# A hybrid decoder step on one core: which engine issues the last stores of the mLSTM and of the prompt attention, and which engine reads out the attention's last result

## The chip, the cores and the metric

The kernel runs on one core of one Trainium2 chip. The metric is the time of the core on the device in microseconds (us), as the median of several executions. The profile is of one execution, with its own time.

## The reference

One inference step of a decoder layer, for a new sequence of 2048 tokens ("prompt") and for 8 x 8 new tokens with a paged past of 8192 positions each ("sample"). Cut to what matters:

```python
z = x @ w_in                                   # one projection for everything
fq, fk, fv, flogf = heads of z                 # FoX attention: 8 heads of 64
mq, mk, mv, ig, lf, og = heads of z            # mLSTM: 4 heads of 128, after a short convolution
fox_h = softmax(fq fk^T / 8 + L_i - L_j, causal) fv     # L = cumulative log forget gate
(C, n, m), m_h = scan over chunks of the mLSTM # matrix memory C, normaliser n
mn  = norm(m_h) * mlstm_norm_w * sigmoid(og)
x1  = layer_norm(ALPHA * x + concat(fox_h, mn) @ w_o)
y   = layer_norm(ALPHA * x1 + relu(x1 @ w1)^2 @ w2)
return y, keys, values, log forget values, C, n, m, convolution state  (prompt and sample)
```

All in 32-bit floats. The kernel gives a product of two 32-bit operands as three products of their high and low parts.

## The kernel before

The program is one long stream of tiles; each engine gets a queue of its own, and a planner of the library orders each engine's queue before the run by its own model of the times (program order is a priority there, not a rule). At run time each queue is in order: an instruction that waits holds up everything behind it on its engine. That includes the instructions that issue DMAs: SyncE (SP in the profile) issues most of them, ScalarE (ACT) and GpSimd (POOL) a few.

The stages, with the engines that matter:

- **Projections and mLSTM** (`block_a`, `m_block`, until about 868 us). Four blocks of 512 tokens. For each, the weights are loaded and split into high and low parts (`split_hi` on ScalarE, L153; `split_lo` on VectorE, L156), TensorE multiplies, results are staged and stored. ScalarE stores the last values of the last block (L604). Beside this runs the mLSTM over chunks of 128 tokens. For each chunk `norm_out` (L628) normalises the result and keeps a function `turn` (L641), which later turns it on TensorE (L644), copies it from PSUM on ScalarE (L646) and stores it to dmix, the buffer of the output projection's input (L647). Behind the last chunk `m_block` stores the state C (L749) and n (L752, by way of a small VectorE copy, L751) and calls `turn_out` for the last chunk. The sampled tokens' decode attention (gathers of pages by GpSimd, L1727 and L1838; its products L1750 and L1862) is spread over the whole kernel.
- **Prompt attention** (`phase_b`, about 868 to 1310 us). 8 heads, 8 units per head, each unit a pair of query tiles. `queries` (L956) loads and splits a pair of queries, `keys` (L938) a group of 512 keys, `forget_values` (L932, L933) the row nl of cumulative forget values, broadcast to all partitions, and the values vn. The first keys and queries (kn0, qn0) are loaded early by `begin_b`. `scores` multiplies (L981, L982), adds nl (L989; L993 with the mask tile nd that GpSimd makes, L974) while it reads PSUM. `values` takes the exponent (L1010), turns the weights (L1026), copies them out on ScalarE or VectorE (L1029, L1031) and multiplies with vn (L1036) into two halves of po. ScalarE copies the first half to ot (L1041), VectorE adds the second (L1043). After every fourth unit `finish` sends the reciprocal sums through DRAM (L1056, L1059), GpSimd multiplies two halves of 512 columns (L1061), and each is stored to dmix (L1062).
- **Output projection** (`phase_o`, from about 1310 us). `mix` loads a token tile of dmix (L1200) and splits it to mh and ml; `weights` splits w_o (first half loaded ahead, L1145); `begin` loads x to y (L1227); `unit` multiplies three times for each of eight slices (L162, L163, L164: high with high, high with low, low with high) and adds.
- **MLP** (`phase_c`, to the end), the longest stage, in which TensorE is the bound.

Tiles of a later stage lie over those of an earlier one, and the library lets an instruction wait for the last reader of each tile that its own tile covers. Between projections and attention, and between attention and output projection, all pools are exchanged.

Of the kernel before, what the change touches and what calls it, by code (L numbers as in the profile page):

```python
# [25 lines left out]
S = 2048  # L26
# [26 lines left out]
def body(ctx, tc, I, O, stages):  # L53
    nc = tc.nc
    V, A, G, T, SY = nc.vector, nc.scalar, nc.gpsimd, nc.tensor, nc.sync
# [12 lines left out]
    dmix = drm.tile([8, 128, TOT], F32, name="dmix")  # L68
# [553 lines left out]
    dmv = dmix.rearrange("j p t -> p j t")  # L622
# [3 lines left out]
    def norm_out(hh, np_, og, tok0, eng=None):  # L626

        st = pm.tile([128, 4, 6], F32, name="st6", bufs=2)  # L628
        mv = pm.tile([128, 4, 2], F32, name="mv2", bufs=2)
        for h in range(4):  # L630
            V.bn_stats(st[:np_, h], hh[:, h])
            V.bn_aggr(mv[:np_, h], st[:np_, h])
        r = pm.tile([128, 2, 4], F32, name="r4", bufs=2)
        V.tensor_scalar(r[:np_, 0], mv[:np_, :, 1], EPS, None, op0=OP.add)
        G.tensor_tensor(r[:np_, 1], r[:np_, 0], nhalf[:np_, 0:4], op=OP.pow)
        for h in range(4):
            V.tensor_scalar(hh[:, h], hh[:, h], mv[:np_, h, 0:1], r[:np_, 1, h:h + 1], op0=OP.subtract, op1=OP.mult)
        hf = hh.rearrange("p h e -> p (h e)")
        (eng or G).tensor_tensor(hf, hf, og, op=OP.mult)

        def turn():  # L641
            po = ppm.tile([128, 4, 128], F32, name="mm", tag="mm", bufs=2)
            for h in range(4):
                T.transpose(po[:, h, :np_], hh[:, h], ident[:np_, :np_])  # L644
            ot = pm.tile([128, 4, 128], F32, name="ot", bufs=1)
            A.copy(ot[:, :, :np_], po[:, :, :np_])  # L646
            SY.dma_start(dmv[:, 4:8, tok0:tok0 + np_], ot[:, :, :np_])  # L647
        mst["turn"] = turn

    def turn_out():  # L650
# [12 lines left out]
    def m_load(c, after=None):  # L663

        def load(dst, src):
            r = SY.dma_start(dst, src)
            if after is not None:
                tc.add_manual_dep(r.ins, after.ins.name,
                                  mybir.DependencyInfo(mybir.DependencyClass.Sync, mybir.DependencyReason.DATA), reason="gates")

        t0 = c * 128
        va = pm.tile([128, 4, 129], F32, name="va", bufs=2)
        G.memset(va[:, :, 128], 1.0)
        SY.dma_start(va[:, :, 0:128], dv[t0:t0 + 128].rearrange("t (h e) -> t h e", h=4))
        Wq = pm.tile([128, 2, 4, 128], F32, name="Wq", bufs=1)
        load(Wq.rearrange("p n h t -> p (n h t)"), dap(dMa, c * 1024, [[0, 128], [1, 1024]]))
        return va, Wq[:, 0], Wq[:, 1]

    def m_block(bi):

        if bi == 0:
            mst["C"] = pm.tile([128, 4, 129], F32, name="Cs", bufs=2)
            V.memset(mst["C"], 0.0)
        gsb = pm.tile([128, 4, 4], F32, name="gsb", bufs=2)
        va, Wm, qa = m_load(bi * 4, mst["gates"])
        SY.dma_start(gsb, dap(dgs, bi * 4, [[0, 128], [16, 4], [1, 4]]))
        for _ in range(4):
            yield 1
        A.activation(gsb, gsb, AF.Exp)
        for c in range(bi * 4, bi * 4 + 4):  # L690
            Cs = mst["C"]
            t0 = c * 128
            qk = mst["qk"][:, c % 4]
            yield 1
            for h in range(4):
                A.activation(Wm[:, h], Wm[:, h], AF.Exp, bias=gm[:, c, h:h + 1], scale=-1.0)
            G.affine_select(Wm, Wm, pattern=[[0, 4], [1, 128]], compare_op=OP.is_ge, fill=0.0, base=0, channel_multiplier=-1)
            A.activation(qa, qa, AF.Exp)
            G.tensor_tensor(qa, qa, qk[:, 0:4], op=OP.mult)
            den = pm.tile([128, 4], F32, name="den", bufs=2)  # L700
            A.activation(den, gm[:, c, 4:8], AF.Exp, scale=-1.0)
            pS = ppm.tile([128, 4, 128], F32, name="mm", tag="mm", bufs=2)
            for h in range(4):
                T.matmul(pS[:, h], qk[:, 4 + h], qk[:, h], start=True, stop=True)
            wk = pm.tile([128, 4], F32, name="wkc", bufs=2)
            G.tensor_copy(wk, Wm[:, :, 127])
            V.scalar_tensor_tensor(Wm, pS, KSC, Wm, op0=OP.mult, op1=OP.mult)
            yield 1
            while bi not in gated:
                yield 1  # L710
            og = pm.tile([128, 512], F32, name="og", bufs=1)
            SY.dma_start(og, dog[t0:t0 + 128])
            yield 1
            turn_out()
            pk = ppm.tile([128, 4, 128], F32, name="mm", tag="mm", bufs=2)
            for h in range(4):
                T.transpose(pk[:, h], qk[:, 4 + h], ident)
            kw = pm.tile([128, 4, 128], F32, name="kw", bufs=1)
            for h in range(4):
                V.tensor_scalar(kw[:, h], pk[:, h], wk[:, h:h + 1], KSC, op0=OP.mult, op1=OP.mult)  # L720
            hh = pm.tile([128, 4, 128], F32, name="hh", bufs=1)
            for p in range(2):
                yield 1
                pn = ppm.tile([128, 2, 129], F32, name="mn", tag="mm", bufs=2)
                for i in range(2):
                    h = 2 * p + i
                    T.matmul(pn[:, i], Wm[:, h], va[:, h], start=True, stop=False)
                    T.matmul(pn[:, i], qa[:, h], Cs[:, h], start=False, stop=True)
                h_out(pn, 2 * p, den[:, 2 * p:2 * p + 2], 128, hh)
            Cn = pm.tile([128, 4, 129], F32, name="Cs", bufs=2)  # L730
            va_ = va
            for p in range(2):
                yield 1
                pc = ppm.tile([128, 2, 129], F32, name="mn", tag="mm", bufs=2)
                for i in range(2):
                    T.matmul(pc[:, i], kw[:, 2 * p + i], va_[:, 2 * p + i], start=True, stop=True)
                for i in range(2):
                    h = 2 * p + i
                    V.scalar_tensor_tensor(Cn[:, h], Cs[:, h], gsb[:, h, c % 4:c % 4 + 1], pc[:, i], op0=OP.mult, op1=OP.add)
                if p == 0:  # L740
                    norm_out(hh, 128, og, t0, V if c == 15 else None)
                    if c % 4 < 3:
                        va, Wm, qa = m_load(c + 1)
            mst["C"] = Cn
        mst["open"] = False
        if bi < 3:
            return
        Cs = mst["C"]
        SY.dma_start(O["C_prompt"][0, 0].rearrange("h d e -> d h e"), Cs[:, :, 0:128])  # L749
        nn = pm.tile([128, 4], F32, name="nn", tag="sm", bufs=1)  # L750
        V.tensor_copy(nn, Cs[:, :, 128])  # L751
        SY.dma_start(O["n_prompt"], nn)  # L752
        yield 1
        turn_out()

# [126 lines left out]
    for bi in range(4):  # L882
        g = block_a(bi)
# [20 lines left out]
    def phase_b():  # L904
# [95 lines left out]
        def values(z, g, sc):  # L1000
# [12 lines left out]
            po = ppb.tile([128, 256], F32, name="po", bufs=1)  # L1013
# [24 lines left out]
            if g % 4 == 0:  # L1038
                z["ot"] = pb.tile([64, 1024], F32, name="ot", bufs=2)
            od = z["ot"][:, (g % 4) * 256:(g % 4) * 256 + 256]  # L1040
            A.copy(od, po[0:64])  # L1041
            q0 = 128 if g == 0 else 0
            V.tensor_tensor(od[:, q0:], od[:, q0:], po[64:128, q0:], op=OP.add)  # L1043
            if g % 4 == 3:
# [2 lines left out]
        def finish(z, half):  # L1047

            h, ls, ot = z["h"], z["ls"], z["ot"]
            lr = pb.tile([128, 32], F32, name="lr", bufs=2)  # L1050
            V.reciprocal(lr, ls)
            lt = pb.tile([128, 32], F32, name="lt", bufs=2)
            V.transpose(lt, lr)
            o = half * 1024
            for a in range(4):
                SY.dma_start(drl[h, o:o + 1024].rearrange("(t a q) -> a t q", a=4, q=32)[a], lt[a * 32 + half * 8:a * 32 + half * 8 + 8])  # L1056
            for q in range(2):
                rl = pb.tile([64, 512], F32, name="rl", bufs=2)
                SY.dma_start(rl, dap(drl, h * S + o + q * 512, [[0, 64], [1, 512]]))  # L1059
                s = slice(q * 512, (q + 1) * 512)  # L1060
                G.tensor_tensor(ot[:, s], ot[:, s], rl, op=OP.mult)  # L1061
                SY.dma_start(dmix[h // 2, (h % 2) * 64:(h % 2) * 64 + 64, o + q * 512:o + q * 512 + 512], ot[:, s])  # L1062

        kns = [pb.tile([128, 512], F32, name="kn", bufs=3)]
        homes = {}
# [2 lines left out]
        units = [(h, g) for h in range(8) for g in range(8)]  # L1068
# [14 lines left out]
        for n in range(len(units) + LA):  # L1083
# [7 lines left out]
            if n < len(units):  # L1091
                h, g = units[n]
# [11 lines left out]
            if n >= LA:  # L1104
                h, g = units[n - LA]
# [5 lines left out]
    dmv = dmix.rearrange("j p t -> p j t")  # L1111
# [898 lines left out]
```

## Time and profile before

| | us |
|---|---|
| median of 3 runs | 3209.95 |
| lowest and highest of these | 3205.98, 3212.35 |
| the profiled execution | 3212.34 |
| its span in the trace | 3210.6 |
| TensorE (PE) busy | 3115.6 (97% of the span) |
| VectorE (DVE) busy | 2080.9 (65%) |
| ScalarE (ACT) busy | 1442.2 (45%) |
| GpSimd (POOL) busy | 902.6 (28%) |

How to read the lines of the profile: a row of the timeline has the start and the length in us, the engine (SPq, ACTq and POOLq are DMA issues), the line of the program, the operation, the tile written and the tiles read, the shape and the count; at the end, in brackets, how long the engine had been idle and what ended that. A row of the busy times by stretch has the stretch, its length, the busy time and the count of instructions of PE, PEld (weight loads), DVE, ACT and POOL, then the clock granted to TensorE (1.00 is full), the mean busy share of the 16 DMA engines and GB/s. A row of waits has who waited, for what, us in total, how often, and the longest. A row of a tile's instructions has the durations in ns (shortest, median, longest) and the first and last start.

### The profile page before, as it was taken

How to read it: one execution, taken by the hardware profiler on the slowest of the kernel's cores; microseconds unless marked ns; L12 is line 12 of the kernel's file. 1: busy time of each engine (PE TensorE's matmuls, PEld its weight loads, DVE VectorE, ACT ScalarE, POOL GpSimd, SP SyncE). 2: the span in 40 equal slices, each digit the busy share in tenths (PEclk: the TensorE clock that was granted, in tenths of full speed). 3: DMA queues.
4: the chain of work that ended last, by engine and by line, in shares of the span. 5: the costliest groups of instructions: out<-in, count | busy, mean ns of one | idle time of the engine just before them, and what ended most of it. 6: DMA issues, size and time to landing. Idle time of an engine off the chain costs nothing. (4 is left out here: it accounts for less than half of the span.)

```text
span 3210.6 us, 55049 instructions
## 1 busy us (share of the span) xinstructions
PE 3115.6 (97%) x20445; PEld 2475.3 (77%) x20445; DVE 2080.9 (65%) x5046; ACT 1442.2 (45%) x2654; POOL 902.6 (28%) x973
## 2 busy tenths in 40 slices
PE   8999999999899999999999999999999999899998
PEld 8997797888767667777677777777767777698886
DVE  6957556465488788534557568556675665766667
ACT  3343343333277777412444445343444444344442
POOL 0121223423333333376333323334333111000000
PEclk9999999999999999999999999999999999999999
DMA  5565766866777865687887869878879866643231
GB/s 190 156 216 179 253 210 211 295 238 228 238 241 189 204 170 138 223 295 257 300 289 269 308 234 322 319 260 307 292 260 340 288 209 204 211 165 131 98 126 63
DMA packets 325075, 732.67 MB, mean 228 GB/s; under 512 B 63592, under 2 KB 161384, under 8 KB 323912
## 3 DMA queue, kind: packets, MB, share of 16 engines
q1 hardware_dynamic: 237672, 414.67, 39.8%
q0 software_dynamic: 83520, 304.12, 27.3%
q10 hardware_dynamic: 3616, 10.36, 0.9%
q8 instruction: 162, 2.65, 0.3%
q14 instruction: 105, 0.86, 0.1%
HBM read 676.20 MB, written 86.38 MB: 238 GB/s over the span
## 5 line engine op out<-in xcount | busy, mean ns | idle before, releaser
L156 DVE TENSOR_TENSOR wl<-wr,wh 128x1024 fp32r<-128x1024 f32 x300 | 365.9, 1223 | 244.0 <-ACT wh L153 204.8
L153 ACT ACTIVATE wh<-wr 128x1024 fp32r<-128x1024 f32 x300 | 315.3, 1055 | 332.0 <-PE py L164 123.7
L162 PE MATMUL ph<-x1h,wh 128*128 128x512 f32 (+1 forms) x1280 | 455.4, 356 | 0.0
L163 PE MATMUL ph<-x1l,wh 128*128 128x512 f32 (+1 forms) x1280 | 453.7, 355 | 0.2 <-DVE x1l L156 0.2
L164 PE MATMUL ph<-x1h,wl 128*128 128x512 f32 (+1 forms) x1280 | 451.7, 355 | 0.2
L1727 POOL DMA_INDIRECT kT<-cache_k,idxK x256 | 277.0, 1082 | 551.9 <-PE sQ L1750 483.2
L162 PE MATMUL py<-wh,hh 128*128 128x512 f32 x900 | 358.9, 403 | 10.1 <-issue 3.6
L163 PE MATMUL py<-wl,hh 128*128 128x512 f32 x900 | 354.5, 395 | 0.2 <-issue 0.2
L164 PE MATMUL py<-wh,hl 128*128 128x512 f32 x900 | 351.8, 395 | 0.4 <-DVE hl L156 0.4
L1376 DVE TENSOR_TENSOR y<-y,py 128x512 f32<-128x512 f32 x410 | 277.2, 683 | 108.4 <-PE py L164 83.0
L1838 POOL DMA_INDIRECT vt<-cache_v,idxV x164 | 178.9, 1091 | 401.4 <-PE sO L1862 341.5
L162 PEld LDWEIGHTS ph<-x1h,wh 128*128 128x128 f32 x1280 | 241.4, 189 | 40.6 <-issue 8.2
L164 PEld LDWEIGHTS ph<-x1h,wl 128*128 128x128 f32 x1280 | 240.8, 189 | 36.5 <-issue 3.7
L163 PEld LDWEIGHTS ph<-x1l,wh 128*128 128x128 f32 x1280 | 241.5, 189 | 34.9 <-issue 3.7
L162 PE MATMUL pm<-whi,xh 128*128 128x256 f32 (+2 forms) x816 | 238.2, 292 | 8.0 <-ACT whi L153 7.9
L163 PE MATMUL pm<-wlo,xh 128*128 128x256 f32 (+2 forms) x816 | 233.9, 287 | 1.0 <-DVE wlo L156 0.6
L164 PE MATMUL pm<-whi,xl 128*128 128x256 f32 (+2 forms) x816 | 234.1, 287 | 0.0
L162 PE MATMUL pm<-xh,whi 128*128 128x512 f32 (+2 forms) x640 | 230.5, 360 | 0.0
L164 PE MATMUL pm<-xh,wlo 128*128 128x512 f32 (+2 forms) x640 | 227.4, 355 | 0.0
L163 PE MATMUL pm<-xl,whi 128*128 128x512 f32 (+2 forms) x640 | 226.8, 354 | 0.0
L162 PEld LDWEIGHTS py<-wh,hh 128*128 128x128 f32 x900 | 169.3, 189 | 66.1 <-issue 25.8
L164 PEld LDWEIGHTS py<-wh,hl 128*128 128x128 f32 x900 | 170.7, 190 | 40.3 <-issue 2.3
(364 smaller groups left out, 6545.2 us busy)
## 6 DMA issues: line engine op xcount, KB each, us to landing
wr<-w SPq DMA_DIRECT2D x200, 512.0 KB
wra<-w_in SPq DMA_DIRECT2D x104, 512.0 KB
wr<-dw SPq DMA_DIRECT2D x96, 512.0 KB
dw<-w POOLq DMA_DIRECT2D x48, 512.0 KB
Rb<-dR SPq DMA_DIRECT2D x128, 128.0 KB
kT<-dw SPq DMA_DIRECT2D x28, 512.0 KB
kT<-w SPq DMA_DIRECT2D x25, 512.0 KB
xn<-xp_t SPq DMA_DIRECT2D x16, 512.0 KB
```

The source lines that it names most:

```text
L153: last["ACT"] = A.activation(dst, src, AF.Copy, scale=scale)
L156: r = (eng or V).tensor_tensor(dst, src, hi.bitcast(F32), op=OP.subtract)
L162: T.matmul(ps, wh, xh, start=first, stop=False, skip_group_check=shared)
L163: T.matmul(ps, wh, xl, start=False, stop=False, skip_group_check=shared)
L164: last["PE"] = T.matmul(ps, wl, xh, start=False, stop=stop, skip_group_check=shared)
L1376: V.tensor_tensor(y, y, ps, op=op)
L1727: G.indirect_dma_start(out=piece(n), out_offset=None, in_=ck, in_offset=IO(ap=idxK[:, b, j // 2, j % 2:j % 2 + 1], axis=0))
L1838: vx["last"] = G.indirect_dma_start(out=vt.rearrange("p f c -> p (f c)"), out_offset=None, in_=cv, in_offset=IO(ap=idxV[:, b, (kt % 4) * 4 ...
```

## The change

Four stores and one copy get another engine; what is computed stays the same.

- The store of the last mLSTM chunk to dmix (L647, only for the last 128 prompt tokens) and the stores of C and n (L749, L752) are issued by ScalarE instead of SyncE.
- The two stores of the last half of the last head (L1062, head 7, half 1) are issued by GpSimd instead of SyncE.
- For the last unit of the attention alone, the copy of po to ot (L1041) is made by VectorE instead of ScalarE.

```diff
@@ norm_out, turn
-            SY.dma_start(dmv[:, 4:8, tok0:tok0 + np_], ot[:, :, :np_])
+            (A if tok0 == S - 128 else SY).dma_start(dmv[:, 4:8, tok0:tok0 + np_], ot[:, :, :np_])
@@ m_block, behind the last chunk
-        SY.dma_start(O["C_prompt"][0, 0].rearrange("h d e -> d h e"), Cs[:, :, 0:128])
+        A.dma_start(O["C_prompt"][0, 0].rearrange("h d e -> d h e"), Cs[:, :, 0:128])
         nn = pm.tile([128, 4], F32, name="nn", tag="sm", bufs=1)
         V.tensor_copy(nn, Cs[:, :, 128])
-        SY.dma_start(O["n_prompt"], nn)
+        A.dma_start(O["n_prompt"], nn)
@@ values
-            A.copy(od, po[0:64])
+            if (z["h"], g) == units[-1]:
+                V.tensor_copy(od, po[0:64])
+            else:
+                A.copy(od, po[0:64])
@@ finish
-                SY.dma_start(dmix[h // 2, (h % 2) * 64:(h % 2) * 64 + 64, o + q * 512:o + q * 512 + 512], ot[:, s])
+                (G if (h, half) == (7, 1) else SY).dma_start(dmix[h // 2, (h % 2) * 64:(h % 2) * 64 + 64, o + q * 512:o + q * 512 + 512], ot[:, s])
```

## The prediction

> **What bounds the kernel now.** I read the page's first part, then the busy times by stretch around the two places that the diff touches, then the timeline of each engine there and SyncE's own waits.
>
> ```profile
> span 3210.6 us, 55049 instructions
> PE 3115.6 (97%) x20445; PEld 2475.3 (77%) x20445; DVE 2080.9 (65%) x5046; ACT 1442.2 (45%) x2654; POOL 902.6 (28%) x973
> 863.00:867.00 4.00, 3.75 (x32) 3.55 (x32) 2.92 (x9) 0.37 (x1) 2.54 (x4) 1.00 0.29 60
> 867.00:871.00 4.00, 1.53 (x7) 0.99 (x5) 1.55 (x7) 1.42 (x3) 0.29 (x1) 0.81 0.90 304
> 871.00:875.00 4.00, 0.00 (x0) 0.00 (x0) 0.00 (x0) 0.00 (x0) 0.00 (x0) 0.50 1.09 250
> 875.00:878.00 3.00, 0.00 (x0) 0.00 (x0) 0.94 (x8) 0.37 (x2) 1.47 (x4) 0.50 0.85 226
> 1310.00:1312.00 2.00, 0.08 (x1) 0.08 (x1) 1.47 (x3) 2.00 (x3) 1.32 (x2) 1.00 0.15 33
> 1312.00:1320.00 8.00, 6.38 (x15) 4.81 (x16) 7.67 (x7) 4.60 (x5) 3.69 (x2) 0.57 0.88 292
> 1320.00:1328.00 8.00, 8.00 (x36) 6.46 (x35) 1.38 (x2) 0.57 (x1) 0.00 (x0) 1.00 1.05 404
> ```
>
> TensorE is busy for 97% of the span; it idles 95 us in all, so only what shortens one of its gaps pays. The diff touches two gaps. At the **first seam** (mixing projections and mLSTM end, prompt attention begins) TensorE does nothing from 871 to 878, and its granted clock is 0.50. There the DMA engines are the bound: share 1.09 and 0.85, though only 0.29 between 863 and 867. At the **second seam** (attention ends, output projection begins) TensorE has 0.08 us of work between 1310 and 1312, and then runs at a mean clock of 0.57 until 1320.
>
> The first seam, from the timeline and SyncE's queue:
>
> ```profile
> 862.69 1.18 SPq L1734 DMA_DIRECT2D Rb<-dR  x2
> 865.94 0.34 ACTq L604 DMA_DIRECT2D v_prompt<-st  x1
> 867.14 0.39 SPq L749 DMA_DIRECT2D C_prompt<-Cs  x1
> 867.34 0.59 ACT L646 COPY ot<-mm 128x512 f32<-128x512 f32 x1 [1.43 <-PE mm L644]
> 867.62 0.72 SPq L752 DMA_DIRECT2D n_prompt<-nn  x1
> 867.82 0.42 ACT L153 ACTIVATE qh<-qn 128x256 fp32r<-128x256 f32 x1
> 868.43 0.63 SPq L647 DMA_DIRECT2D dmix<-ot  x1
> 869.12 0.68 SPq L932 DMA_DIRECT2D nl<-dnl  x1
> 869.92 0.42 PE L982 MATMUL pS<-ks,ql 128*128 128x256 f32 x1
> 874.23 0.34 SPq L932 DMA_DIRECT2D nl<-dnl  x1
> 875.23 2.38 SPq L956 DMA_DIRECT2D qn<-dq  x4
> 876.53 1.69 POOL L974 TENSOR_TENSOR nd<-nl,dmask 128x128 f32<-128x128 f32 x4 [8.70 <-DMA nl<-dnl]
> 877.02 0.29 DVE L993 CUSTOM_DVE_ANT_0 S<-pS,nd 128x128 f32<-128x128 f32 x1 [7.54 <-POOL nd L974]
> 879.19 0.96 ACT L153 ACTIVATE qh<-qn 128x256 fp32r<-128x256 f32 x2
> SPq L749 <- DVE pad_4x L84: 3.6, 1, 3.6
> SPq L932 <- DMA v_prompt<-st: 2.6, 1, 2.6
> SPq L933 <- DMA C_prompt<-Cs: 0.2, 1, 0.2
> L457 PE MATMUL mg<-ident,rows x17: 169/198/199, 64.4 to 710.0; 4*128 4x4 f32 x16, 4*64 4x4 f32 x1
> ```
>
> SyncE has nothing to issue after 863.87: it stands at the C_prompt store until the state is done (867.14; 3.6 us, put down to a later VectorE instruction), issues three stores, and only then the forget row nl of the first query pair. That row reaches GpSimd at 876.53, 7.4 us after its issue at 869.12; the scores that wait for it were done by 870.4. So the first pair waits for nl alone. The **second pair** hangs elsewhere: its queries are the first two of the four qn loads at 875.23, behind the second nl, which stood 2.6 us until the landing of the v_prompt store that ScalarE had issued at 865.94 (to 874.23), and behind the second vn, which waited 0.2 us for C_prompt's landing. Counted in issue order, nl is the eighth DMA behind v_prompt, and vn the eighth behind C_prompt: each DMA waits until the one eight before it has landed. ScalarE splits these queries only at 879.19.
>
> **The change, part by part.** *Three stores from SyncE to ScalarE.* Taken off SyncE: the 3.6 us stand and 0.39 + 0.72 + 0.63 = 1.74 us of issue. What the first nl waits for apart from its place in the queue the trace doesn't show; its bounds are 863.9 (right behind Rb) and 867.4 (869.12 less 1.74). In the program before, its tile lies over buffers of the gate computation (rows), which is read last at 710, so I take 863.9. With the same 7.4 us it lands at 871.3. vn and two kn loads follow at once.
>
> Put on ScalarE: the same 1.74 us. C_prompt waits for the state (867.14), and behind it stands the copy of ot, which started at 867.34 in any case; this wait costs nothing, nor does n_prompt's for its small copy by VectorE. But qh, until now at 867.82, starts about 869.6, the key split and first scores slip with it by 1.74 us, and the first score pair ends at 870.34 + 1.74 = 872.1. Now nl (871.3) is no longer last: the scores are. The first pair's eviction moves from 877.02 to about 872.2, 4.8 us earlier. If nl did not move, the 1.74 us would still be hidden, since 872.1 is under 876.5.
>
> The second pair gains less. Its queries still stand behind the landings of v_prompt, C_prompt, the small n_prompt and dmix, the eight-before rule with the same eight. These bytes are the same; what changes is that the first nl, vn and kn can use the DMA engines between 865 and 867, where the share is 0.29. Filled, that is 0.71 x 2 = 1.4 us of their work, and the 0.10 left over in the next 4 us another 0.4. So everything behind lands up to 1.8 us earlier. I take **-1.8 us** for the seam. Upper end: both pairs as early as the first, -4.8 us. Lower end: the stores land later in ScalarE's queue. The v_prompt store took 874.23 - 865.94 = 8.3 us there; with ScalarE issuing dmix near 869 and the same 8.3 us, its landing is 877.3, and the second half of the queries, issued at 875.8 until now (0.6 us each from 875.23), goes at 877.3: +1.5 us.
>
> The Trainium skill speaks against a gain here: DMA: Bandwidth & Descriptors, section "Issuing engines are not separate DMA queues", says that transfers started by several engines run on the same 16 DMA engines, and that a second issuer saves only the time of issuing. The full stretch from 871 to 875 agrees, the 3.6 us stand at an in-order head doesn't. By that rule alone the seam would give 0, and the time would be rival C's.
>
> The second seam:
>
> ```profile
> 1305.44 1.13 ACT L1029 COPY PT<-pt 128x384 f32<-128x384 f32 x2 [0.20 <-PE pt L1026]
> 1305.88 3.67 PE L1036 MATMUL po<-PT,vn 128*64 128x256 f32 x32
> 1308.57 3.69 SPq L1062 DMA_DIRECT2D dmix<-ot  x2
> 1309.60 0.37 ACT L1041 COPY ot<-po 64x256 f32<-64x256 f32 x1 [3.03 <-PE po L1036]
> 1309.87 1.05 ACT L153 ACTIVATE mh<-xr 128x1024 fp32r<-128x1024 f32 x1
> 1310.00 0.42 DVE L1043 TENSOR_TENSOR ot<-ot,po 64x256 f32<-64x256 f32 x1 [4.30 <-ACT ot L1041]
> 1310.50 1.27 POOL L1061 TENSOR_TENSOR ot<-ot,rl 64x512 f32<-64x512 f32 x1 [1.96 <-DVE pad_5x L84]
> 1310.96 1.90 DVE L156 TENSOR_TENSOR ml<-xr,mh 128x1024 fp32r<-128x1024 f32 x1 [0.53 <-ACT mh L153]
> 1311.92 0.50 PE L162 MATMUL pw<-wh,mh 128*128 128x512 f32 x1 [2.38 <-ACT wh L153]
> 1312.31 2.77 SPq L1227 DMA_DIRECT2D y<-x_prompt  x5
> 1314.05 0.80 PE L163 MATMUL pw<-wl,mh 128*128 128x512 f32 x1 [1.62 <-DVE wl L156]
> 1242.76 0.83 POOL L1140 DMA_DIRECT2D dw<-w  x1
> 1341.63 1.05 PE L1862 MATMUL sO<-vx,PTs 128*32 128x256 f32 x16
> ```
>
> *The last result read by VectorE.* ScalarE loses the 0.37 us copy, and, what weighs more, its 3.03 us wait for TensorE's last product. It is then free at 1306.6, and the splits mh and wh run from there (in its row mh follows the copy without an idle time of its own), so the first product wh can follow the last po matmul at 1309.6, 2.3 us earlier. VectorE gets a copy of the same 64x256 form; the row nearest to it is its own add of that form, 0.42 us. It starts when the product is there, 1309.6, and the add ends at 1310.4 as before. The second product needs wl, and that VectorE makes in order behind the add and ml. ml waited for mh until 1310.96; now it starts right behind the add and the tiny pad, 1310.45. So wl, and the second product, come 0.5 us earlier: TensorE fills in one product early and then stands again. **-0.5 us**; half-clock running until 1320 stays in this sum.
>
> *The last stores by GpSimd.* SyncE loses a stand of 1308.57 to 1312.26. The first y load may then go at once, the others partly wait for buffers that the last multiply (to 1311.77) reads, bounds 1305.4 and 1312.3. These loads fill DMA engines that have a share of 0.15 at 1310 to 1312, and the w_o loads behind them move up too; but TensorE is full from 1320 to 1328 with what it has (8.00 of 8.00), so I price that at 0, with -1 us as the far end. GpSimd gets two issues of 0.83 us each (its own plain DMA row). The first lies in its idle 1.96 us; the second delays the two gathers behind it by 0.8 us, and their data is read at 1341.63, so 0, with +0.8 as the far end.
>
> Sum: -1.8 - 0.5 = -2.3 us. The profiled execution took 3212.34 (span 3210.6 and 1.7 around it), 2.4 above the median of the three runs shown. Against the median: 3209.95 - 2.3 = **3207.7 us**.
>
> **The rivals.** *A, the whole chain comes forward and the clock stays up.* Both first pairs gain 4.8 us; and at the second seam the gap stays too short for the clock to fall. The fifteen products from 1314.05 to 1320 are 0.40 us apart; at full clock, as the 36 in the 8 us after show, they would be 0.22 apart: 15 x 0.18 = 2.7 us less. -4.8 - 0.5 - 2.7 = -8.0: 3202.0. For it: the stand of SyncE is real, and the clock fell to 0.50 only after the 1311.92 product. Against it: the eight-before waits, and wl still comes late. TensorE: Matmul & The Clock Gate, Part 1 of the Trainium skill, has the clock halve after one idle window of about 3.4 us that runs free of the kernel; the gap here, 1310 to 1313.5, is just that long, so by the rule the clock may stay up: this rival's second half.
>
> *B, slower: SyncE waits for ScalarE's stores.* The mechanism is the lower end of the first seam: the landing of dmix decides, and the point is 875.8. Each us that it lands after that goes straight into the second pair's queries and, as SyncE issues in order, into the keys and rows of the pairs behind, while TensorE stays at half clock. +1.5 for 877.3, less 0.5: 3211.0. If the delay comes back in each of the next rounds of eight, five of them at most before both pairs' heads are loaded, it reaches 7.5 - 0.5 = +7.0: 3217.
>
> *C, no effect.* Order in each queue is fixed before the run, and instructions do stand out of program order there (five y loads in a row at 1312.31); if nl keeps its place in time, ScalarE's 1.74 us stay hidden and only the second seam counts: 3209.5.
>
> **How the numbers follow.** Forecast 0.4, A 0.2, B 0.2, C 0.2. A change under 0.2%, 6.4 us, is about what a measurement of this kernel can't tell from none (its three runs lie 6.4 us apart). Faster by over 0.2% is most of A and the fast edge of the forecast: 0.24. Slower is B's upper half and a little of the rest: 0.14. Within: 0.62. The range takes in A and B's middle and the spread of the runs: 3200 to 3214.
>
> **What would show it.** Right: nl issued before 866 and landed by 872; qh on ScalarE near 869.6; the first eviction near 872; the second pair's qh near 877.4; mh before 1308 and the second pw product near 1313.5. Wrong: nl still behind the state's end; C_prompt or dmix landing after 876; a changed order of TensorE's products later on, which none of these sums holds.

## The result and the profile after

The changed kernel takes **3219.2 us** (median of 20 runs, 3205.0 to 3231.28), the kernel before, run beside it, 3206.74 us (20 runs, 3197.84 to 3214.67). The ratio is 1.0041, 95% interval 1.0031 to 1.0052: 13.1 us slower (9.9 to 16.7), where 2.3 us less was forecast; the median also lies above the forecast range (3200 to 3214). The profiled execution took 3216.09 us, against 3212.34 of the one before; so the two traces are 3.75 us apart in all, and the place of the loss has to be read from marks near the two seams. Line numbers behind the read-out are three higher than before.

The head of the page after:

```profile
span 3214.4 us, 55049 instructions
PE 3110.5 (97%) x20445; PEld 2475.9 (77%) x20445; DVE 2085.0 (65%) x5047; ACT 1443.6 (45%) x2653; POOL 907.0 (28%) x975
```

The totals say nothing: TensorE is busy for 97% here too. The **first seam** after, from the timelines of SyncE, ScalarE, TensorE, GpSimd and VectorE:

```profile
861.17 0.58 SPq L932 DMA_DIRECT2D nl<-dnl  x1
861.80 0.43 SPq L933 DMA_DIRECT2D vn<-v_prompt  x1
863.20 0.34 ACTq L604 DMA_DIRECT2D v_prompt<-st  x1
866.83 0.42 ACT L153 ACTIVATE qh<-qn 128x256 fp32r<-128x256 f32 x1
868.92 0.41 PE L982 MATMUL pS<-ks,ql 128*128 128x256 f32 x1
869.25 1.69 POOL L974 TENSOR_TENSOR nd<-nl,dmask 128x128 f32<-128x128 f32 x4 [4.17 <-DMA nl<-dnl]
869.74 0.29 DVE L993 CUSTOM_DVE_ANT_0 S<-pS,nd 128x128 f32<-128x128 f32 x1 [1.25 <-POOL nd L974]
873.48 0.33 SPq L932 DMA_DIRECT2D nl<-dnl  x1
878.56 0.42 ACT L153 ACTIVATE qh<-qn 128x256 fp32r<-128x256 f32 x1 [3.48 <-DMA qn<-dq]
```

The stage ahead of the seam ended 2.74 us sooner in this execution (v_prompt store at 863.20 against 865.94), so count from that store. The first nl goes out 2.0 us ahead of it (3.2 behind it before), and the first eviction comes 6.5 us behind it (11.1 before). That part came out about as planned, though the scores were not the last to come: they were done at 869.33, and the eviction waited 0.4 us more for the mask that GpSimd makes from nl, from 869.25 on. But the second nl comes 10.3 us behind it (8.3 before), and the second pair's queries 15.4 (13.3 before). SyncE's waits between 860 and 880 us say for what:

```profile
SPq L932 <- DMA v_prompt<-st: 7.4, 1, 7.4
```

It is the same wait as before, for the same store, and it was 2.6 us then. The **second seam**, each engine's timeline in turn (VectorE, GpSimd, SyncE, ScalarE, TensorE):

```profile
1313.69 0.42 DVE L1042 COPY ot<-po 64x256 f32<-64x256 f32 x1 [3.90 <-PE po L1036]
1314.14 0.42 DVE L1046 TENSOR_TENSOR ot<-ot,po 64x256 f32<-64x256 f32 x1
1314.49 1.22 DVE L156 TENSOR_TENSOR ml<-xr,mh 128x1024 fp32r<-128x1024 f32 x1
1315.63 4.62 DVE L156 TENSOR_TENSOR wl<-wr,wh 128x1024 fp32r<-128x1024 f32 x4
1320.17 1.21 DVE L156 TENSOR_TENSOR ml<-xr,mh 128x1024 fp32r<-128x1024 f32 x1
1321.30 1.21 DVE L156 TENSOR_TENSOR wol<-wr,woh 128x1024 fp32r<-128x1024 f32 x1
...
1314.64 9.02 POOL L1064 TENSOR_TENSOR ot<-ot,rl 64x512 f32<-64x512 f32 x1 [1.23 <-DVE pad_5x L84]
...
1309.56 15.96 SPq L1230 DMA_DIRECT2D y<-x_prompt  x5
1325.57 0.64 SPq L1203 DMA_DIRECT2D xr<-dmix  x1
1326.25 5.26 SPq L1148 DMA_DIRECT2D wr<-w_o  x3
...
1338.09 1.06 ACT L153 ACTIVATE woh<-wr 128x1024 fp32r<-128x1024 f32 x1 [20.80 <-DMA wr<-w_o]
...
1313.56 0.50 PE L162 MATMUL pw<-wh,mh 128*128 128x512 f32 x1
1316.90 0.50 PE L163 MATMUL pw<-wl,mh 128*128 128x512 f32 x1 [2.83 <-DVE wl L156]
...
1339.20 0.80 PE L162 MATMUL pw<-woh,mh 128*128 128x512 f32 x1 [6.94 <-ACT woh L153]
```

GpSimd's last multiply took **9.02 us**; before it took 1.27. Above it stands the reason: VectorE went from the addition straight into seven subtractions without a gap, 1314.49 to 1322.51, and the multiply, begun 0.15 us behind the first of them, ended 1.15 us behind the last. The chain from there: five y loads that took 2.77 us now span 15.96, because of one wait in SyncE's queue (waits between 1305 and 1345 us):

```profile
SPq L1230 <- POOL ot L1064: 11.4, 1, 11.4
```

The y row of token tile 1 lies over the buffer that this multiply reads. Behind it stand the loads of the second half of w_o; ScalarE waits 20.80 us for one (10.83 before); and TensorE, which went straight through before, waits 6.94 us for ScalarE and then runs with a lowered clock. The busy times by stretch, after and then before:

```profile
1330.00:1340.00 10.00, 3.06 (x23) 1.83 (x16) 0.82 (x1) 1.06 (x1) 1.88 (x2) 0.73 1.04 396
1340.00:1348.00 8.00, 8.00 (x26) 6.38 (x26) 3.45 (x4) 2.11 (x2) 0.00 (x0) 0.70 1.05 407
```

```profile
1330.00:1340.00 10.00, 10.00 (x48) 8.01 (x50) 4.98 (x9) 2.22 (x3) 3.80 (x3) 1.00 0.95 371
```

10.00 us of TensorE work in that stretch became 3.06, at a clock of 0.73, and in the next stretch the clock is still 0.70. The prediction priced a late load there at nothing, since TensorE was full from 1320 to 1328.

### The profile page after: what moved, and what is told of

Its sections match the earlier page's. It is cut to its first block, busy times and chain, and to the rows that moved or that the text cites. A ratio compares the mean times of both kernels' runs of the same rounds, so it can differ in the third digit from the quotient of the medians.

```text
span 3214.4 us, 55049 instructions
## 1 busy us (share of the span) xinstructions
PE 3110.5 (97%) x20445; PEld 2475.9 (77%) x20445; DVE 2085.0 (65%) x5047; ACT 1443.6 (45%) x2653; POOL 907.0 (28%) x975
```

## The experiments

The theory after this look, **L (lock-out)**: the read-out on VectorE frees ScalarE, so mh is early, so VectorE's run begins before GpSimd's multiply instead of behind it. Rivals: **G**, the two stores on GpSimd are to blame; **M**, the three stores on ScalarE are. Each kernel is compared with runs of the kernel before beside it, whose median lay at 3217.35, 3209.89 and 3217.84 us in the first three groups of runs; the kernels with one run were run for their trace.

The table holds, for each, two marks of the first seam (issue of the second nl, and start of the 701st matmul behind the first score product, both from the end of the copy that fills the last v_prompt store) and three of the second (the last multiply; issue of the third w_o load and start of the 91st matmul behind the attention's last product), in us from the trace, and the time against the kernel before with its 95% interval.

| | second nl | 701st | multiply | w_o | 91st | time, us |
|---|---|---|---|---|---|---|
| before | 8.3 | 125.6 | 1.27 | 12.3 | 25.3 | |
| after | 10.3 | 129.7 | 9.02 | 16.6 | 32.6 | +13.1 (+9.9 to +16.7) |
| e1_readout | 8.2 | 125.1 | 9.02 | 20.9 | 34.7 | +9.7 (+5.8 to +13.5) |
| e2_gstores | 8.1 | 125.3 | 1.26 | 9.1 | 24.1 | +0.3 (-3.2 to +3.9) |
| e3_actstores | 10.7 | 127.7 | 1.26 | 12.6 | 24.0 | +2.3 (-1.6 to +6.1) |
| e4_vmult | 9.8 | 127.7 | 0.68 | 6.2 | 23.4 | +4.2 (+0.3 to +8.0) |
| e5_mstores_g | 1.3 | 125.9 | 1.27 | 12.5 | 23.8 | -3.5 (-8.0 to +1.0) |
| e6_best | 1.8 | 125.4 | 0.68 | 6.5 | 24.8 | -6.4 (-10.9 to -1.6) |
| e7_longrun | 8.4 | 125.2 | 10.15 | 21.4 | 36.2 | |
| e8_seam2 | 7.9 | 124.4 | 0.68 | 6.8 | 23.5 | -1.6 (-6.1 to +3.2) |
| e9_yload | 10.5 | 127.0 | 7.89 | 5.5 | 23.9 | +1.3 (-2.3 to +4.8) |
| e10_noread | 8.2 | 124.2 | 0.68 | 6.8 | 23.3 | |
| e11_ring | 1.3 | 125.3 | 1.27 | 12.4 | 25.0 | |

The 91st mark also carries a stretch of half clock that begins 3 to 5 us behind the attention's last product in every trace. It lasts 6.8 us in the kernel before, e6 and e11 (24.8 to 25.3) and 3.4 us in the others; those of them without a late w_o load lie at 23.3 to 24.1.

**One part at a time.** e1_readout, the kernel before with:

```diff
-            A.copy(od, po[0:64])
+            if (z["h"], g) == units[-1]:
+                V.tensor_copy(od, po[0:64])
+            else:
+                A.copy(od, po[0:64])
```

> The kernel before with the read-out of the attention's last result on VectorE, and nothing else. Theory L (lock-out): with ScalarE free early, mh is ready when VectorE has finished the last result, so VectorE goes from the addition straight into its run of seven subtractions (ml, four wl, ml, wol), and GpSimd's last multiply, which reads and writes SBUF, is kept out until the run is over: in the profile after it took 9.02 us where it took 1.27 us before. Here too it takes 8 to 10 us, its store to dmix and every load behind that on SyncE goes out that much later, the second woh split comes about 10 us later, and the time is 8 to 11 us above the kernel before. Rival G (the GpSimd stores are to blame, by what they cost GpSimd or by what SyncE then issues ahead): the multiply stays at 1.3 us and the time within 2 us of the kernel before. Rival M (the mLSTM's stores are to blame): the same, within 2 us.

Measured: ratio 1.003 (1.0018 to 1.0042), +9.7 us. GpSimd's and SyncE's timelines of this run:

```profile
1317.29 9.02 POOL L1064 TENSOR_TENSOR ot<-ot,rl 64x512 f32<-64x512 f32 x1 [2.11 <-DVE pad_5x L84]
...
1315.20 11.60 SPq L1065 DMA_DIRECT2D dmix<-ot  x2
```

The same 9.02 us, with all stores where they were; here SyncE stands at the store behind the multiply instead of at the y load. One copy of 0.42 us costs 9.7 us.

e2_gstores, the kernel before with the two last stores on GpSimd:

```diff
-                SY.dma_start(dmix[h // 2, (h % 2) * 64:(h % 2) * 64 + 64, o + q * 512:o + q * 512 + 512], ot[:, s])
+                (G if (h, half) == (7, 1) else SY).dma_start(dmix[h // 2, (h % 2) * 64:(h % 2) * 64 + 64, o + q * 512:o + q * 512 + 512], ot[:, s])
```

> The kernel before with the attention's last two stores to dmix on GpSimd, and nothing else. Theory L: ScalarE still reads the last result out, so VectorE still waits for mh between the addition and its first subtraction, as before (0.53 us); the multiply gets in first and takes 1.3 to 2 us; the time is within 3 us of the kernel before. Rival G: 8 to 12 us above it, with the w_o loads on SyncE late. Rival M: within 2 us.

Measured: 1.0001 (0.999 to 1.0012). G falls.

e3_actstores, the kernel before with the first seam's part:

```diff
-            SY.dma_start(dmv[:, 4:8, tok0:tok0 + np_], ot[:, :, :np_])
+            (A if tok0 == S - 128 else SY).dma_start(dmv[:, 4:8, tok0:tok0 + np_], ot[:, :, :np_])
-        SY.dma_start(O["C_prompt"][0, 0].rearrange("h d e -> d h e"), Cs[:, :, 0:128])
+        A.dma_start(O["C_prompt"][0, 0].rearrange("h d e -> d h e"), Cs[:, :, 0:128])
-        SY.dma_start(O["n_prompt"], nn)
+        A.dma_start(O["n_prompt"], nn)
```

> The kernel before with the mLSTM's last three stores on ScalarE, and nothing else. Theory L: the second seam is as before (multiply 1.3 us), and only the first seam changes. By the profile after, where the products from 888 us on stood 2.6 to 3.6 us later against those before the seam, that costs 2 to 4 us: 3208.7 to 3210.7 if the kernel before runs at 3206.7. The prediction's own sum for this seam was a gain of 1.8 us. Rival M: 8 to 12 us above the kernel before.

Measured: 1.0007 (0.9995 to 1.0019), +2.3 us; by the time alone it may also be nothing. Its trace has the late second nl again, with this row among SyncE's waits:

```profile
SPq L932 <- DMA v_prompt<-st: 8.1, 1, 8.1
```

M falls as the main cause. The three parts add up: 9.7 + 0.3 + 2.3 = 12.3, against 13.1 for the whole.

**Taking the lock-out away.** e4_vmult, the changed kernel with:

```diff
-                G.tensor_tensor(ot[:, s], ot[:, s], rl, op=OP.mult)
+                (V if (h, half, q) == (7, 1, 1) else G).tensor_tensor(ot[:, s], ot[:, s], rl, op=OP.mult)
```

> The changed kernel with the last multiply (second half of the last pair of rows) on VectorE, directly behind the addition, so that GpSimd has nothing to read against VectorE's run. Theory L: the multiply takes about 0.7 us, the last store goes out some 9 us sooner than in the changed kernel, the w_o loads with it, and 8 to 11 us of the loss are gone: within 4 us of the kernel before, and 8 to 12 us below the changed kernel. Rivals G and M: no more than 2 us below the changed kernel, 10 us or more above the kernel before.

Measured: 1.0013 (1.0001 to 1.0025), +4.2 us. About 9 of the 13 us are gone, on the edge of what L expected (within 4). The multiply takes 0.68 us, the w_o loads go out 8.5 to 10.4 us sooner than in the changed kernel, and the 91st product comes at 23.4. By the marks, what is left stands at the first seam. e8_seam2 has the same second seam (stores on GpSimd, read-out and multiply on VectorE) with the mLSTM's stores back on SyncE:

> The kernel before with the second seam's edits alone and the lock-out taken away: last stores on GpSimd, last result read out by VectorE, last multiply on VectorE; the mLSTM's stores stay on SyncE. By the run that had the same second seam and the mLSTM's stores on ScalarE, phase O's 91st product came 23.4 us after the last product of the attention, 24.0 in the two runs without the read-out on VectorE at the same clock: 0.5 to 1.5 us below the kernel before, and 2 to 4 us below the run with the ScalarE stores if the first seam is what was left of the loss.

Measured: 0.9995 (0.9981 to 1.001), -1.6 us; the step from e4 to e8 is as expected in sign, 5.8 us by the two middles (2 to 4 expected), each good to some 4 us.

**Does the lock-out last as long as VectorE's run?** e7_longrun is e1 with three subtractions more behind the run, each a repetition of ml of token tile 1:

```diff
             split_lo(ml, mr, mh, eng)
+            if t == 1:
+                for _ in range(3):
+                    split_lo(ml, mr, mh)
             return mh, ml
```

> The kernel before with the read-out on VectorE, and ml of the second token tile computed four times instead of once (three subtractions more, each the same as the first, all of two SBUF inputs). Lock-out for the whole run: two of the three stand directly behind the run of seven, which ended 8.9 us after the last product of the attention, so the multiply, 9.02 us long with seven, becomes 10.1 us if the small bubble between two dependent subtractions lets it in, and 11.3 us if it doesn't. If the 9 us are something else of the multiply's own (its data, its transfer, a fixed stall), it stays at 9.0 us. The time is not of interest.

The run's end and the multiply, from VectorE's and GpSimd's timelines:

```profile
1324.46 1.21 DVE L156 TENSOR_TENSOR ml<-xr,mh 128x1024 fp32r<-128x1024 f32 x1
1325.59 1.21 DVE L156 TENSOR_TENSOR wol<-wr,woh 128x1024 fp32r<-128x1024 f32 x1
1326.73 3.44 DVE L156 TENSOR_TENSOR ml<-xr,mh 128x1024 fp32r<-128x1024 f32 x2
...
1318.93 10.15 POOL L1064 TENSOR_TENSOR ot<-ot,rl 64x512 f32<-64x512 f32 x1 [2.04 <-DVE pad_5x L84]
```

10.15 us with eight subtractions in a row, the first of the two branches: 9.02 + 1.13. The ninth depends on the eighth, and at that point GpSimd got in: the two repetitions span 3.44 us, two of 1.14 and the multiply's 1.15 between. So it isn't a property of the multiply; it waits for the first bubble in VectorE's run.

**Where the price is paid.** e9_yload is the changed kernel, lock-out and all, with one load on another engine:

```diff
-            SY.dma_start(xs[t], x_of(t))
+            (A if t == 1 else SY).dma_start(xs[t], x_of(t))
```

> The changed kernel with one load moved from SyncE to ScalarE: the row y of token tile 1, whose buffer lies over the one that GpSimd's last multiply reads, and at which SyncE stood 11.4 us in the changed kernel with the w_o loads behind it. The lock-out stays. Theory P (the price is paid through SyncE's queue): the three w_o loads go out 4 to 7 us after the last product of the attention (12.6 to 16.6 in the changed kernel, 6.3 to 12.3 in the kernel before), phase O's 91st product comes at 24 to 26 us (32.6 and 25.3), and the time is 1 to 5 us above the kernel before, what the first seam costs. ScalarE now stands at that load, so VectorE's seventh subtraction, which needs ScalarE's next split, can't follow the sixth: the run has six, and the multiply takes 9.02 - 1.13 = 7.9 us. Rival D (the price is paid by the data of the locked-out multiply, or on GpSimd): the 91st product stays at 31 us or later and the time 8 us or more above the kernel before.

Its timelines (VectorE, GpSimd, SyncE):

```profile
1322.95 1.21 DVE L156 TENSOR_TENSOR ml<-xr,mh 128x1024 fp32r<-128x1024 f32 x1
1326.89 1.22 DVE L156 TENSOR_TENSOR wol<-wr,woh 128x1024 fp32r<-128x1024 f32 x1 [2.73 <-ACT woh L153]
...
1317.42 7.89 POOL L1064 TENSOR_TENSOR ot<-ot,rl 64x512 f32<-64x512 f32 x1 [1.04 <-DVE pad_5x L84]
...
1319.65 2.60 SPq L1148 DMA_DIRECT2D wr<-w_o  x3
```

Measured: 1.0004 (0.9993 to 1.0015), +1.3 us. The multiply is still locked out, for a run that is now six long (7.89 us, 7.9 expected), but the w_o loads go out at 3 to 6 us and the 91st product comes at 23.9. P holds: nobody on the path needs the multiply soon; what costs is SyncE, standing at it with the weights behind.

e10_noread takes the stores on GpSimd and the multiply on VectorE, and lets ScalarE read the last result out, as before:

> The kernel before with the last multiply on VectorE and the attention's last stores on GpSimd; ScalarE reads the last result out, as before. Beside the run that has the read-out on VectorE too (phase O's second product 4.0 us after the last product of the attention, its 91st at 23.5, with one half-clock window of 3.4 us), this gives the price of the read-out alone, which the prediction put at 0.5 us: second product at 4.5, 91st at 24.0 with the same clock. If ScalarE's early splits are worth more, by filling the gap, the 91st comes at 25 or later.

Second product at 3.9 us (4.0 with the read-out on VectorE), 91st at 23.3 (23.5); 4.5 and 24.0 were expected. With the lock-out gone, the read-out is worth nothing that these marks show; each is from one trace.

**The first seam.** e5_mstores_g is the kernel before with four stores off the shared rotation: the last v_prompt store and the mLSTM's three.

```diff
-                (A if bi == 3 and i == 1 else SY).dma_start(d, stage(ps, m, 256))
+                (G if bi == 3 and i == 1 and t == 15 else A if bi == 3 and i == 1 else SY).dma_start(d, stage(ps, m, 256))
-        SY.dma_start(O["C_prompt"][0, 0].rearrange("h d e -> d h e"), Cs[:, :, 0:128])
+        G.dma_start(O["C_prompt"][0, 0].rearrange("h d e -> d h e"), Cs[:, :, 0:128])
...
```

> The kernel before with the mLSTM's last three stores and the last v_prompt store (t 15) in front of them on GpSimd, and nothing else: they leave the rotation of eight semaphores that SyncE's and ScalarE's DMAs share. Theory R (rotation): in the changed kernel the first seam's second pair of loads waits for the landing of the v_prompt store, which went out behind the 1 MB of loads that SyncE now issues first: second nl issue 10.3 us after that store, 8.3 before, and the products after the seam 2.3 us later (128 us after the store, runs with the stores on ScalarE against runs without). With the store off the rotation the second nl goes out within 4 us of the store, the second pair of scores 3 us or more sooner than before, and the products after the seam 2 to 5 us sooner than in the kernel before: time 2 to 5 us below it. Rival T (traffic: the second pair is late because the stores and loads share the transfer time, whatever waits for what): the second nl may go out early but lands no sooner; within 1.5 us of the kernel before, or above it.

The store on GpSimd and the second nl, from the two timelines:

```profile
868.65 0.61 POOL L604 DMA_DIRECT2D v_prompt<-st  x1 [0.46 <-ACT st L486]
...
869.62 0.88 SPq L932 DMA_DIRECT2D nl<-dnl  x1
```

R's first half is right: the second nl goes out 1.3 us behind the store's data, not 8.3. Its second half is wrong. TensorE's and ScalarE's rows of this run, then the row of the kernel before where the second pair's scores begin:

```profile
876.26 1.19 PE L1026 MATMUL pt<-ident,S 128*128 128x128 f32 x3 [3.43 <-ACT S L1010]
881.06 1.08 PE L1036 MATMUL po<-PT,vn 128*64 128x256 f32 x4 [3.61 <-issue]
882.07 1.54 PE L981 MATMUL pS<-ks,qh 128*128 128x384 f32 x3
...
879.15 0.63 ACT L153 ACTIVATE ks<-kn 128x512 fp32r<-128x512 f32 x1 [2.44 <-DMA kn<-k_prompt]
881.43 0.80 ACT L153 ACTIVATE qh<-qn 128x256 fp32r<-128x256 f32 x2 [1.49 <-DMA qn<-dq]
```

```profile
879.65 1.11 PE L981 MATMUL pS<-ks,qh 128*128 128x384 f32 x2
```

Two rows of the busy times by stretch, of e5 and of the changed kernel:

```profile
870.00:880.00 10.00, 2.02 (x7) 1.02 (x7) 2.54 (x13) 2.98 (x9) 4.04 (x10) 0.62 1.03 287
```

```profile
873.00:875.00 2.00, 0.02 (x1) 0.03 (x1) 0.54 (x1) 1.20 (x4) 0.00 (x0) 0.50 0.22 46
```

Counted from the store's data (868.35 in this run, 865.91 before), TensorE comes to the first pair's turns 4.4 us sooner, but then stands 3.61 us, and the second pair's scores begin at 13.7 us, as before. The first of their queries is issued at 3.0 us instead of 9.3 and yet split at 13.1 instead of 13.3: ScalarE waited for it to land. That is what T expected of the loads: they go out early and land hardly sooner, with the DMA engines full from 870 to 880 us (share 1.03). The 701st product comes at 125.9, and the time, 0.9989 (0.9975 to 1.0003), agrees with a gain and with none. In the changed kernel it was the wait: when SyncE got to issue the second nl at 873.48, the DMA engines had little left to do (share 0.22 from 873 to 875). So a late second pair costs here, by the marks of the four kernels with the stores on ScalarE (the second pair's scores begin at 15.1 to 15.9 us there); what an early one would bring this run doesn't show, since it had none.

e11_ring asks why the v_prompt store landed late: the mLSTM's three stores on GpSimd, the v_prompt store alone on ScalarE.

> The kernel before with the mLSTM's last three stores on GpSimd; the last v_prompt store stays on ScalarE, alone there. SyncE's first nl (256 KB) and vn (128 KB; not 1 MB, as an earlier expectation said) go out ahead of that store, as in the changed kernel. Question: why the v_prompt store landed 10.3 us after its data was ready in the changed kernel and 8.3 in the kernel before. If the loads that now go out ahead of it are the reason, it still lands 9.8 us or more behind. If it is the C, n and dmix stores that follow it on ScalarE's queue, it lands by 8.4 us. The rotation moves on by three, so that the second nl doesn't wait for it; the queries of the first pair's second tile do.

SyncE's waits in this run (L956 is a load of queries):

```profile
SPq L956 <- DMA v_prompt<-st: 6.4, 1, 6.4
```

With three stores off the shared rotation the wait moved on by three loads, from the second nl to the second qn, as a count of eight says. The store landed 10.55 us behind its data (7.9 to 8.4 in the six kernels that keep SyncE's order; 9.8 to 10.7 in the four with the stores on ScalarE). The stores behind it on ScalarE's queue are therefore not the reason. That it is the loads issued ahead of it is what remains of the two; the loads that follow it at once in this run are not separated from them.

**All of it together.** e6_best is e5 with e8's second seam:

> The kernel before with all of that (the four stores of the first seam on GpSimd), the attention's last two stores on GpSimd, its last result read out by VectorE, and the last multiply on VectorE. If R and the lock-out are both right: the gain of the run with the four stores alone plus 0.5 to 2 us at the second seam, so 3 to 7 us below the kernel before. If T: 0 to 2 us below it.

Measured: 0.998 (0.9966 to 0.9995), -6.4 us: faster than the kernel before, and the only kernel here whose interval lies below it. That lies within the 3 to 7 us expected if R and the lock-out both held, but R's gain isn't in its marks: the second pair's scores begin at 13.75 us, as before, the 701st product comes at 125.4, and the 91st at 24.8. So the agreement of the number proves nothing for R, and the place of the gain is open.

## Why the prediction was wrong, point by point

- **First nl ahead of the state's end: right in size, not in what ends the wait.** Issue before 866 was asked for; it came 2.0 us ahead of the v_prompt store. ScalarE's queries slipped by 1.75 us against the store (1.74 forecast), hidden as said, and the first eviction moved by 4.5 us (4.8 forecast). But the forecast had the scores last. In the trace nl took 8.1 us from its issue to GpSimd instead of 7.4, and the mask made from it, which the sum left out, came 0.4 us behind the scores. That the sum was off by no more is luck.
- **The second pair, -1.8 us: wrong in sign.** The step that failed: "These bytes are the same ... everything behind lands up to 1.8 us earlier". The second nl waits for the landing of the v_prompt store, and the loads that the edit freed now go out ahead of that very store. It landed 2.0 us later (whether through the loads ahead of it or those behind, e11 leaves open); the 701st product came at 127.0 to 129.7 us in the four kernels with the stores on ScalarE, and at 124.2 to 125.6 in the six that keep SyncE's order. In time the part alone is +2.3 us (e3), with an interval that takes in 0. Rival B had the mechanism, SyncE waiting for a store of ScalarE's, and a near size (+1.5), but the wrong store: dmix. The Trainium skill's DMA: Bandwidth & Descriptors, section "Issuing engines are not separate DMA queues", which the prediction weighed, would have given 0 here; the marks lie on the slower side of that, and e3's interval takes it in.
- **The early splits: right.** mh began 3.1 us ahead of the last product's end, the first product came 2.45 us sooner behind it (2.3 forecast), the second 1.24 us (0.5 forecast); the other 0.7 us is ml, 1.22 us instead of 1.90 since the multiply no longer runs beside it.
- **The read-out, -0.5 us: +9.7 in e1.** The failed step is the one that gave this gain: "now it starts right behind the add". It was worked out for ml and not followed to GpSimd, whose multiply waits for the same addition. The prediction had quoted the warning: ml took 1.90 us beside the multiply, while the subtractions in the changed kernel take 1.21 to 1.22. In the kernel before, ml's wait of 0.53 us for ScalarE let the multiply begin first; that idle time was what the edit removed. The Trainium skill's SBUF — State Buffer, section "Who interferes with whom", has the rule: a VectorE instruction with two SBUF inputs and a GpSimd instruction that reads SBUF exclude each other, and the second waits. The runs agree, with 1.27 us against 9.02, and go further than the sentence there: the second waited for seven instructions, not for one.
- **GpSimd's stores and SyncE's early y loads, 0: half right.** e2 gives 0.3 us. But "the w_o loads behind them move up too" held only as long as no y load waits for the late multiply; it was named as a reader of those buffers, and its time was taken as fixed.
- **The clock (rival A): not seen.** In every trace a half-clock stretch begins 3 to 5 us behind the attention's last product, after included (3.4 us long, 6.8 before). In TensorE's wait for the late w_o load a second one begins there, 10.2 us long.
- **The range.** It ended at 3214 because the only slower case, B, was priced at the first seam and taken in to its middle alone. The bound for the second seam ended at +0.8 us for gathers. A bound for a later multiply, worked through SyncE's queue to the w_o loads, was missing.

## What to carry to other kernels

When a wait is removed, ask which other engine was let in by it: an idle 0.5 us on VectorE was GpSimd's entry here, and closing it cost 9.7 us. Where an instruction on a shared resource gets later, follow its buffers too: the multiply's result was not urgent, but a load into the memory it reads stood at the head of the queue that brings the weights. And when loads are freed to go early, look for what they overtake: a store whose landing the next loads wait for.

## What the runs showed of the hardware that was not expected

GpSimd is not kept out by every run of subtractions. Where its multiply had been on first, the gather of pages that follows got in during the same run; where the multiply is on VectorE, the gather was kept out until the end. GpSimd's rows in e2_gstores, then in e8_seam2:

```profile
1313.31 1.26 POOL L1061 TENSOR_TENSOR ot<-ot,rl 64x512 f32<-64x512 f32 x1 [1.18 <-DVE pad_5x L84]
...
1315.74 1.99 POOL L1838 DMA_INDIRECT vx<-cache_v,idxV  x1 [0.31 <-ACT wh L153]
```

```profile
1315.58 0.56 POOL L1065 DMA_DIRECT2D dmix<-ot  x1 [1.84 <-DVE pad_5x L84]
1316.45 7.74 POOL L1841 DMA_INDIRECT vx<-cache_v,idxV  x1 [0.31 <-ACT mh L153]
```

The gather took 1.85 to 1.99 us in the kernel before, e2, e3 and e5, and 7.1 to 7.74 us in e4, e6, e8 and e10, in each case beside a run of seven. A plain store that GpSimd issues (0.56 us) was not held up. Why the gather gets in at the end of one subtraction in the one case and only behind the last in the other, no run here separates. The marks of e4, e8 and e10 show no price for it.
